# Turning the second half's rows by transposing DMA and a ScalarE weave instead of by TensorE

## The chip, the cores and the metric

The kernel runs on one core of a Trainium2 chip. The metric is the device time of one execution in microseconds (us), taken as the median of several runs: 1520.02 us before the change, over three runs from 1519.76 to 1521.08. One further execution was profiled; every trace number below is from that one.

Engines are named as in the profile: PE is TensorE (matmul; PEld its weight loads), DVE is VectorE, ACT is ScalarE, POOL is GpSimd, and SP is SyncE, which here issues most of the transfers. SPq and ACTq are the instruction queues of SP and ACT, where transfers are issued.

## The reference, cut to what matters

One layer of a hybrid decoder trunk on 1024 tokens of 1024 float32 channels. The first step normalises each token's row and multiplies it by w_in, whose output is cut into eight projections; all of them read the normalised row:

```python
def rms_norm(x, gain):
    y = xf * lax.rsqrt(jnp.mean(xf * xf, axis=-1, keepdims=True) + NORM_EPS)
    return (y * gain.astype(jnp.float32)).astype(x.dtype)

def hybrid_mixer(h, ...):                      # h = rms_norm(x, norm_mix)
    proj = h @ w_in
    xa, ga, q, f, v, g, m_a, m_b = jnp.split(proj, SPLIT_POINTS, axis=-1)
    xa = causal_depthwise_conv(xa, conv_w, conv_b)
    y_a = rg_lru(xa, w_r, b_r, w_i, b_i, lam) * jax.nn.gelu(ga)
    ...                                        # q, f, v: HGRN2 in chunks of 32 tokens, 8 heads of 128
    y = jax.nn.sigmoid(m_a) * y_a + jax.nn.sigmoid(m_b) * y_b
    return y @ w_out
```

Then come a residual sum, a second normalisation, a squared-ReLU MLP of width 4096, another residual and a final normalisation. The change touches only how the normalised rows h of tokens 512 to 1023 get into the layout that the projections read.

## The kernel before

**Layout.** A matmul contracts over the 128 partitions. Rows of x come from memory with tokens on the partitions, so the normalised rows must be turned, channels onto the partitions, before they are multiplied by w_in. The turned rows are held as `hT[c]` for the two token halves c = 0, 1 of 512 tokens each. In float32 each operand is split in two fp32r parts, a high part (an ACT cast, line 97) and a low part (a DVE subtraction, line 101), and a product is three matmuls (`mm3`, line 160). So hT[1] is four tiles: hT10H, hT10L for channels 0 to 511 and hT11H, hT11L for channels 512 to 1023.

**Stages.** The mixers' work is done in eight stages, i = 4c + p for half c and pair p of blocks of 256 channels. Stage i computes v of the pair before (`v_of`), then the projections xa, q and f, and the RG-LRU gates of its own pair, while the HGRN2 chunk work of the pair before is interleaved step by step. The scores of that pair are the short matmuls `sc<-qb,kc` and `sc<-qf,kk` (lines 834 and 845), fed by ACT and DVE. Stage 4 is the first to read hT[1]: its xa projection needs hT10H and hT10L from its first matmuls. All of it sits between about 60 and 500 us of the span; stage 1's xa ends near 75 us, stage 4's begins at 247.7 us.

**Weights.** SP loads each 128x1024 block of weights into one of four `raw` buffers, ACT casts the high part wH, DVE subtracts the low part wL. In the first half wL is also stored to memory (`rest<-wL`), and in the second half reloaded (`wL<-rest`).

**Order.** A scheduler orders the instructions of each engine, guided by the order in which the code calls the pieces, by priorities (`tc.high_priority`) and by added order edges (`held`, line 90, and the like). After that the order on an engine is fixed; an instruction that has to wait holds up all behind it on its engine, and on SP a transfer that has to wait to be issued holds up the transfers behind it.

**The rows of the second half.** Each of the four token tiles of half 1 is loaded and normalised by `next_rows` (line 476): load x (SP), square with sum (ACT, line 185), epsilon (DVE), power (POOL), scale (DVE). Then `transposed` (line 200) turns it: eight PE transposes 128x128 into two banks of PSUM, and `split` writes the high and low parts of both channel halves. Tile 0 is turned after stage 1's xa, tile 1 in stage 2's xa (`hooks` in `stage`), tiles 2 and 3 in stage 3's xa.

## Time and profile before

| what | before |
|---|---|
| median of three runs | 1520.02 us (1519.76 to 1521.08) |
| the profiled execution's own time | 1520.71 us |
| span in the trace | 1518.9 us |
| PE busy | 1508.5 us, 99%, 9035 matmul instructions |
| DVE busy | 1146.9 us, 76% |
| ACT busy | 814.8 us, 54% |
| POOL busy | 155.4 us, 10% |
| PE transposes of `transposed` (line 204) | 32, mean 272 ns each, from 75.6 to 195.9 us |

Busy time is an average over the span. A PE that is busy for nearly all of it says that the other engines' work is hidden behind PE as a whole; where in a stage they are early or late is seen only in the timeline, by comparing when an input is ready with when PE reads it. In a timeline row the columns are start (us), length (us), engine, line, operation, output <- inputs, shape and count; the last bracket, if there is one, is the time that the engine idled before it and what ended that idle time.

### The profile page before, as it was taken

How to read it: one execution, taken by the hardware profiler on the slowest of the kernel's cores; microseconds unless marked ns; L12 is line 12 of the kernel's file. 1: busy time of each engine (PE TensorE's matmuls, PEld its weight loads, DVE VectorE, ACT ScalarE, POOL GpSimd, SP SyncE). 2: the span in 40 equal slices, each digit the busy share in tenths (PEclk: the TensorE clock that was granted, in tenths of full speed). 3: DMA queues.
4: the chain of work that ended last, by engine and by line, in shares of the span. 5: the costliest groups of instructions: out<-in, count | busy, mean ns of one | idle time of the engine just before them, and what ended most of it. 6: DMA issues, size and time to landing. Idle time of an engine off the chain costs nothing.

```text
span 1518.9 us, 23175 instructions
## 1 busy us (share of the span) xinstructions
PE 1508.5 (99%) x9035; PEld 1264.9 (83%) x9035; DVE 1146.9 (76%) x1661; ACT 814.8 (54%) x1369; POOL 155.4 (10%) x191
## 2 busy tenths in 40 slices
PE   9999999999999999999999999999999999999998
PEld 7888988888889888888888888888888888888886
DVE  6889686485585739776756579878888998888877
ACT  5566746656667345645443357666666821111115
POOL 1021120242634600000000000000000000000000
PEclk9999999999999999999999999999999999999999
DMA  7546547466674383442339234666666676666642
GB/s 290 200 176 221 163 171 244 151 230 227 207 241 153 137 307 139 125 139 83 134 116 347 95 125 167 263 249 249 249 249 249 249 278 264 247 249 247 249 184 111
DMA packets 98432, 310.50 MB, mean 204 GB/s; under 512 B 23185, under 2 KB 36625, under 8 KB 85906
## 3 DMA queue, kind: packets, MB, share of 16 engines
q1 hardware_dynamic: 94112, 298.91, 54.4%
q10 hardware_dynamic: 4210, 10.10, 1.8%
q8 instruction: 71, 1.16, 0.3%
q14 instruction: 39, 0.32, 0.1%
HBM read 201.50 MB, written 103.81 MB: 201 GB/s over the span
## 4 chain that ended last, share of the span: by engine, by line
PE 99%; DMA 0%; DVE 0%; ACT 0%; issue 0%; POOL 0%; SPq 0%; POOLq 0%
PE uX L160 11%; PE dX L160 11%; PE gX L160 10%; PE pj_q L160 6%; PE pj_xa L160 6%; PE pj_f L160 6%; PE po L160 6%; PE dY L160 6%; PE uY L160 6%; PE pv L160 5%; PE gY L160 5%; PE uZ L160 3%; PE dZ L160 3%; PE gZ L160 3%; PE g L160 1%; PE mb L160 1%
## 5 line engine op out<-in xcount | busy, mean ns | idle before, releaser
L1916 DVE TENSOR_TENSOR acc<-acc,dX 128x512 f32<-128x512 f32 x128 | 85.1, 684 | 26.7 <-PE dX L160 26.0
L97 ACT CAST wA<-q 128x512 fp32r<-128x512 f32 x46 | 28.6, 622 | 115.9 <-PE dX L160 94.7
L160 PE MATMUL po<-wH,y 128*128 128x512 f32 x256 | 80.6, 391 | 0.0
L101 DVE TENSOR_TENSOR wL<-raw,wH 128x1024 fp32r<-128x1024 f32 x46 | 56.3, 1227 | 31.7 <-ACT wH L97 31.6
L97 ACT CAST wH<-raw 128x1024 fp32r<-128x1024 f32 x46 | 48.1, 1047 | 32.7 <-DMA raw<-wts_in 16.2
L1816 POOL TENSOR_TENSOR gx<-acc,gain 128x256 f32<-128x256 f32 x1 | 0.7, 742 | 604.5 <-DVE acc L1916 604.5
L160 PEld LDWEIGHTS po<-wH,y 128*128 128x128 f32 x256 | 48.1, 188 | 9.8
L1916 DVE TENSOR_TENSOR acc<-acc,dY 128x512 f32<-128x512 f32 x64 | 43.6, 687 | 14.2 <-PE dY L160 13.8
L160 PE MATMUL po<-wL,y 128*128 128x512 f32 x128 | 49.8, 389 | 0.0
L1664 ACT ACTIVATE b<-b 128x512 f32<-128x512 f32 x48 | 30.0, 625 | 29.7 <-DVE b L1663 27.9
L195 POOL TENSOR_TENSOR rstd_h<-rstd_h,mhalf 128x1 f32<-128x1 f32 x8 | 4.3, 545 | 370.2 <-DVE rstd_h L190 370.2
L160 PE MATMUL uX<-h2B11H,wA 128*128 128x512 f32 x128 | 42.1, 390 | 0.0
L101 DVE TENSOR_TENSOR wA<-q,wA 128x512 fp32r<-128x512 f32 x46 | 31.5, 686 | 13.6 <-ACT wA L97 13.6
L606 DVE SCALAR_TENSOR_TENSOR xc<-xp,pvt,xc 128x512 f32<-128x512 f32 x48 | 39.9, 840 | 1.2 <-ACT xc L590 1.1
L123 ACT CAST wH<-raw 128x1024 fp32r<-128x1024 f32 x36 | 37.2, 1044 | 5.6 <-issue 3.1
L160 PE MATMUL gX<-hT00H,wA 128*128 128x512 f32 x112 | 36.8, 390 | 0.0
L1147 DVE TENSOR_TENSOR s<-q,q 128x512 f32<-128x512 f32 x46 | 31.6, 687 | 2.9 <-DMA q<-mlp_in 2.7
L504 POOL TENSOR_TENSOR stt<-r,stt 128x256 fp32r<-128x256 f32 x16 | 21.2, 1348 | 118.8 <-ACT stt L503 107.5
L1155 DVE TENSOR_TENSOR s<-q 128x512 f32<-128x512 f32 x46 | 31.7, 690 | 0.2
L1665 ACT ACTIVATE b<-b 128x512 f32<-128x512 f32 x48 | 30.1, 630 | 1.0
L931 ACT ACTIVATE on<-po 128x128 f32<-128x128 f32 x64 | 16.9, 278 | 24.6 <-PE po L927 24.6
L160 PEld LDWEIGHTS uX<-h2B11H,wA 128*128 128x128 f32 x128 | 24.0, 188 | 5.0
(2328 smaller groups left out, 5285.7 us busy)
## 6 DMA issues: line engine op xcount, KB each, us to landing
q<-mlp_in SPq DMA_DIRECT2D x92, 512.0 KB, 3.6
raw<-wts_in SPq DMA_DIRECT2D x80, 512.0 KB, 4.8
rest<-wL SPq DMA_DIRECT2D x36, 512.0 KB, 3.0
wL<-rest SPq DMA_DIRECT2D x36, 512.0 KB, 4.0
hd<-ri SPq DMA_DIRECT2D x16, 256.0 KB, 3.5
cdT<-stT SPq DMA_DIRECT2D x16, 256.0 KB, 3.1
h<-hd SPq DMA_DIRECT2D x4, 1024.0 KB, 4.7
y<-yd SPq DMA_DIRECT2D x8, 512.0 KB, 9.4
```

The source lines that it names most:

```text
L97: ins = casts[name] = A.copy(h, src)
L101: ins = V.tensor_tensor(out=lo, in0=src, in1=h.bitcast(F32), op=ALU.subtract)
L123: A.copy(h, raw)
L160: ins = PE.matmul(o, a, b, start=begins, stop=ends, **how)
L504: G.tensor_tensor(out=lo, in0=src, in1=h.bitcast(F32), op=ALU.subtract)
L606: ins = V.scalar_tensor_tensor(xc[:, s, :], xp[:, j : j + T], pvt[:, PV_CW + 8 * j + u : PV_CW + 8 * j + u + 1], xc[:, s, :], op0=ALU.mult ...
L931: A.activation(row(s, n), halves_of(po[s][:, n * P : (n + 1) * P]), AF.Square, accum_out=ssq[:, 4 * s + n : 4 * s + n + 1],)
L1147: ins = V.tensor_tensor(out=sa[:, 0, :], in0=a21, in1=a22, op=ALU.add)
L1155: ins = V.tensor_tensor(out=sb[:, 0, :], in0=a21, in1=a11, op=ALU.add)
L1664: A.activation(b[:, at, :], b[:, at, :], AF.Relu, scale=-1.0 if at == 2 else 1.0)
L1665: A.activation(b[:, at, :], b[:, at, :], AF.Square)
L1916: return V.tensor_tensor(out=dst, in0=dst, in1=banks[bk, pr], op=op)
```

## The change

`transposed` is no longer called for these tiles. `next_rows` becomes a generator of four parts that are called one at a time by `row_on(n)`:

1. load x, normalise, and transpose the normalised rows as 2-byte elements by a DMA issued on SP, into a tile `xT`. Each float32 becomes two rows of halves: the low 16 bits and the high 16 bits of one channel stand on separate partitions.
2. store `xT` to memory (`xd`) in two transfers.
3. load it again into `xp` ("parts") in two transfers of 64 partitions, so that both halves of a channel stand on that channel's partition.
4. two ACT copies of 2-byte elements weave the halves back into float32 numbers (`xw`), and `split` writes the high and low parts, now from SBUF.

`xT`, `xw` and the tile that receives x share one buffer (`tile_x`, line 228, tag "xt" with one buffer), so the next tile's x can be loaded only when DVE has read the woven rows of the tile before. `xn` and `xp` share two buffers. The weave is the same operation that the kernel already uses for another tensor at line 1331.

The parts are called at these places: tile 0 at the end of stage 0 (1), in stage 1's xa (2), and in stage 1's q after two steps (3) and after six (4); tile 1 at the end of stage 1 (1), in stage 2's v (2 and 3) and xa (4); tile 2 at the end of stage 2 (1), in stage 3's v (2 and 3) and xa (4); tile 3 in stage 3 before the last steps of f (1 and 2), after the gates (3), and in stage 4's v after its first token tile (4).

```diff
--- before.py
+++ after.py
@@ -148,7 +148,7 @@
         used[0] += 1
         return get_w(used[0] - 1)
 
-    pinned = [False]
+    pinned, newest = [False], [None]
 
     def pin(ins):
         if pinned[0]:
@@ -159,6 +159,7 @@
         for a, b, begins, ends in ((ah, bh, first, False), (ah, bl, False, False), (al, bh, False, last)):
             ins = PE.matmul(o, a, b, start=begins, stop=ends, **how)
             pin(ins)
+            newest[0] = ins
             if chain is not None:
                 edge = mybir.DependencyInfo(mybir.DependencyClass.NoSync, mybir.DependencyReason.DATA)
                 if chain:
@@ -478,7 +479,34 @@
         nc.sync.dma_start(xt, x[(4 + tt) * P : (5 + tt) * P, :])
         xn = xt_pool.tile([P, D], F32, tag="xn", name=f"xn1{tt}", bufs=2)
         norm_rows(xt, xn, gain0[0], f"x1{tt}", behind, square_behind)
-        return xn
+        t = tile_x(f"xT{tt}").bitcast(U16).rearrange("p (j x) -> p j x", x=P)
+        nc.sync.dma_start_transpose(t, xn.bitcast(U16))
+        yield
+        for g in range(2):
+            held(nc.sync.dma_start(xd[tt][:, g], t.rearrange("p (k g) x -> p g k x", g=2)[:, g]), newest[0])
+        yield
+        parts = xt_pool.tile([P, D], F32, tag="xn", name=f"xp1{tt}", bufs=2)
+        parts = parts.bitcast(U16).rearrange("p (h t) -> p h t", h=2)
+        for g in range(2):
+            part = nc.sync.dma_start(
+                parts[64 * g : 64 * g + 64],
+                xd[tt][:, g].rearrange("(a h) k t -> a h (k t)", h=2),
+            )
+            held(part, newest[0])
+        yield
+        whole = tile_x(f"xw{tt}")
+        pairs = whole.bitcast(U16).rearrange("p (t h) -> p h t", h=2)
+        at = slice(tt * P, (tt + 1) * P)
+        with tc.high_priority(400):
+            for h in range(2):
+                cut = slice(h * T, (h + 1) * T)
+                held(A.copy(pairs[:, :, cut], parts[:, :, cut]), newest[0])
+                split(
+                    whole[:, cut].rearrange("p (k t) -> p k t", k=4),
+                    hT[1][0][h][:, :, at],
+                    hT[1][1][h][:, :, at],
+                )
+        yield
 
     def make_combos(i):
         k, cut = i // 2, slice(256 * (i % 2), 256 * (i % 2) + 256)
@@ -949,7 +977,12 @@
         got["normalised"] = normalised
         got["on"] = on
 
-    xn1 = {}
+    xd = [dram.tile([P, 2, 8, P], U16, tag=f"xd{t}", name=f"xd{t}") for t in range(4)]
+    row_parts = {}
+
+    def row_on(n):
+        next(row_parts[n])
+
     where = lambda i: divmod(i, NPAIR)
 
     def hooked(steps, hooks):
@@ -972,9 +1005,8 @@
                 gots[i - 2]["stored"] = on_T(*where(i - 2), gots[i - 2], nc.sync)
             if tt == 3 and i > 1:
                 gots[i - 2]["stored"](nc.scalar.dma_start)
-            for n in {}.get((i, tt), ()):
-                with tc.high_priority(400):
-                    transposed(xn1[n], hT[1], n, f"x1{n}")
+            for n in {(2, 1): (1,), (2, 3): (1,), (3, 1): (2,), (3, 3): (2,), (4, 0): (3,)}.get((i, tt), ()):
+                row_on(n)
 
         yield from v_steps(*where(i - 1), gots[i - 1], between)
 
@@ -984,11 +1016,7 @@
         if i > 1:
             yield from v_of(i)
 
-        def more(n):
-            with tc.high_priority(400):
-                transposed(xn1[n], hT[1], n, f"x1{n}")
-
-        hooks = {at: lambda n=n: more(n) for at, n in {2: ((4, 1),), 3: ((2, 2), (6, 3))}.get(i, ())}
+        hooks = {at: lambda n=n: row_on(n) for at, n in {1: ((6, 0),), 2: ((6, 1),), 3: ((4, 2),)}.get(i, ())}
         px = yield from hooked(project_steps(c, f"xa{c}{p}"), hooks)
         xc, xps = conv_in(c, p, px)
         if i == 0:
@@ -998,20 +1026,24 @@
         yield
         if i == 1:
             gots[0]["tail"]()
-            transposed(xn1[0], hT[1], 0, "x10")
         if i > 4:
             combos_on(2)
 
         def convolve():
             got["xc"] = conv(c, p, xc, xps, None)
 
-        pq = yield from hooked(project_steps(c, f"q{c}{p}"), {} if i == 1 else {6: convolve})
+        hooks = {2: lambda: row_on(0), 6: lambda: row_on(0)} if i == 1 else {6: convolve}
+        pq = yield from hooked(project_steps(c, f"q{c}{p}"), hooks)
         got["q1"] = q_of(c, p, pq)
         yield
         fs = hooked(project_steps(c, f"f{c}{p}"), {6: convolve} if i == 1 else {})
         for _ in range(5 if i > 1 else 7):
             next(fs)
             yield
+        if i == 3:
+            row_parts[3] = next_rows(3, gots[2]["states"])
+            row_on(3)
+            row_on(3)
         if i > 3:
             combos_on(1 if i == 4 else 2)
         if i == 0:
@@ -1023,11 +1055,13 @@
         yield from rg_lru(c, p, got, *got["xc"])
         if i > 0:
             gots[i - 1]["normalised"]()
-        for n in ((0,), (1,), (2, 3))[i] if i < 3 else ():
-            if i == 0:
-                xn1[n] = next_rows(n, behind_first[1], behind_first[0])
-            else:
-                xn1[n] = next_rows(n, gots[0]["states"] if i == 1 else None)
+        if i < 3:
+            row_parts[i] = next_rows(
+                i, behind_first[1] if i == 0 else gots[0]["states"] if i == 1 else None, behind_first[0] if i == 0 else None
+            )
+            row_on(i)
+        if i == 3:
+            row_on(3)
         if i > 1:
             pf = yield from fs
             got["f"], got["kk"] = f_of(c, p, pf)
```

On PE the eight rows `L204 MATMUL xT_x…` are gone and the order is otherwise the same. Three places on the other queues follow. In the names, `wH`, `raw` and `rest` are weight parts as above, `x` is the loaded tile, `xn` the normalised rows, `sq` belongs to the q projection of the stage, `kk`, `kc`, `qb`, `qf` feed the scores of the pair before; line numbers are those of the kernel that the row is from, and differ by about 28 between the two.

ACT in stage 1, before:

```order
L97 CAST hT10H<-xT_x_0_828 128x4x128
L97 CAST hT11H<-xT_x_1_835 128x4x128
L762 COPY seg_721<-seg_721 128x32
L97 CAST wH_911<-raw_909 128x1024
L681 ACT_TABLE_LOAD
L681 ACTIVATE sq_975<-pj_q_0_842 128x512
L97 CAST wH_1043<-raw_1041 128x1024
L681 ACTIVATE sq_975<-pj_q_1_843 128x512
L812 COPY kk_654<-kc_736 128x16x32
L97 CAST xcH_1139<-xc_812 128x1024
L813 COPY qf_1024<-qb_728 128x16x32
L97 CAST wH_1075<-raw_1073 128x1024
```

ACT in stage 1, with the change:

```order
L503 COPY xw_926<-xp_858 128x2x512 x2
L97 CAST hT10H<-xw_926 128x4x128
L97 CAST hT11H<-xw_926 128x4x128
L97 CAST wH_1047<-raw_1045 128x1024
L709 ACT_TABLE_LOAD
L709 ACTIVATE sq_979<-pj_q_0_836 128x512
L709 ACTIVATE sq_979<-pj_q_1_837 128x512
L840 COPY kk_658<-kc_742 128x16x32
L97 CAST xcH_1143<-xc_820 128x1024
L186 ACTIVATE xn_1293,rstd_x_1294<-x_1291 128x1024
L97 CAST wH_1079<-raw_1077 128x1024
L841 COPY qf_1028<-qb_734 128x16x32
```

Ahead of `qf` there are now two weave copies and the square of tile 1's rows (`xn<-x`); the casts of hT follow the weave, and the weight cast `wH_1047`, the table load and both `sq` stand behind them.

SP in stage 1, before (`hd` stores the RG-LRU state rows of a pair):

```order
L129 DMA rest_754<-wL_751 128x1024
L112 DMA raw_1041<-wts_in 128x1024
L129 DMA rest_786<-wL_783 128x1024
L112 DMA raw_1073<-wts_in 128x1024
L129 DMA rest_850<-wL_847 128x1024
L112 DMA raw_1198<-wts_in 128x1024
L670 DMA hd_93<-ri_645 128x512 x2
L129 DMA rest_915<-wL_912 128x1024
L112 DMA raw_1323<-wts_in 128x1024
```

SP in stage 1, with the change:

```order
L486 DMA xd_132<-xT_723 128x8x128
L129 DMA rest_792<-wL_789 128x1024
L486 DMA xd_132<-xT_723 128x8x128
L112 DMA raw_1077<-wts_in 128x1024
L491 DMA xp_858<-xd_132 64x2x1024
L129 DMA rest_844<-wL_841 128x1024
L698 DMA hd_93<-ri_649 128x512 x2
L491 DMA xp_858<-xd_132 64x2x1024
L129 DMA rest_912<-wL_909 128x1024
L112 DMA raw_1202<-wts_in 128x1024
L112 DMA raw_1329<-wts_in 128x1024
L479 DMA x_1291<-x_in 128x1024
```

The two stores to `xd` and the two loads of `xp` are put between the weight transfers, the second load behind both `hd` stores; the load of tile 1's x comes after it.

ACT at the end of stage 3's work and the start of stage 4, before:

```order
L745 COPY kb_2714<-kk_2701 128x512
L662 ACT_TABLE_LOAD
L662 ACTIVATE rw_2630<-rw_2630 128x1024
L123 CAST wH_2745<-raw_2743 128x1024
L123 CAST wH_2869<-raw_2867 128x1024
L762 COPY seg_2711<-seg_2711 128x128
L778 COPY kc_2726<-kb_2714 128x128x2
L782 COPY qb_2718<-qa_2712 128x32x4x2
```

ACT there with the change:

```order
L773 COPY kb_2711<-kk_2698 128x512
L690 ACT_TABLE_LOAD
L690 ACTIVATE rw_2624<-rw_2624 128x1024
L123 CAST wH_2742<-raw_2740 128x1024
L503 COPY xw_2781<-xp_2676 128x2x512 x2
L97 CAST hT10H<-xw_2781 128x4x128
L97 CAST hT11H<-xw_2781 128x4x128
L123 CAST wH_2873<-raw_2871 128x1024
L790 COPY seg_2708<-seg_2708 128x128
L806 COPY kc_2723<-kb_2711 128x128x2
L810 COPY qb_2715<-qa_2709 128x32x4x2
```

Two weave copies and the two casts of hT now stand between the first two casts of reloaded weights, ahead of `seg`, `kc` and `qb`.

## The prediction

> **What bounds the kernel now.** I read the page first: busy share by engine, granted clock, and the chain of work that ended last.
>
> ```profile
> span 1518.9 us, 23175 instructions
> ...
> PE 1508.5 (99%) x9035; PEld 1264.9 (83%) x9035; DVE 1146.9 (76%) x1661; ACT 814.8 (54%) x1369; POOL 155.4 (10%) x191
> ...
> PEclk9999999999999999999999999999999999999999
> ...
> PE 99%; DMA 0%; DVE 0%; ACT 0%; issue 0%; POOL 0%; SPq 0%; POOLq 0%
> ```
>
> The profiled run took 1520.71 us, 1.81 more than its span. TensorE (PE) is busy for 1508.5 us, its granted clock is in the top tenth in every slice, and the chain is PE alone. The next view lists what PE waited for (total, times, longest):
>
> ```profile
> PE gain L336 <- POOL gain_row L326: 2.5, 1, 2.5
> PE xT_x L369 <- DVE xn L360: 0.9, 1, 0.9
> ```
>
> Both waits belong to the kernel's first lines, before the stages. In the stages PE never waits, so only two things move the end: work taken off PE, and a wait that is new for PE. Another engine's work costs something only where its slack before a PE instruction is used up. The change acts in stages 0 to 4, up to about 260 us. One stretch of these, by windows (length, then busy time of PE, PEld, DVE, ACT, POOL, granted clock, DMA share, GB/s):
>
> ```profile
> 60.00:130.00 70.00, 70.00 (x607) 60.14 (x606) 65.40 (x118) 51.20 (x100) 10.10 (x12) 1.00 0.51 174
> ```
>
> DVE is busy for 65 of 70 us and ACT for 51. There is room on average, but both work in order, so what counts is the slack at the places where PE meets them.
>
> **What is removed.** The transposes as a group, then PE's timeline around the first of their four groups:
>
> ```profile
> L204 PE MATMUL xT_x<-ident,xn x32: 270/272/273, 75.6 to 195.9; 128*128 128x128 f32 x32
> ```
>
> ```profile
> 75.10 0.39 PE L160 MATMUL pj_xa<-hT01L,wH 128*128 128x512 f32 x1
> 75.33 0.39 PE L160 MATMUL pj_xa<-hT01H,wL 128*128 128x512 f32 x1
> 75.56 1.03 PE L204 MATMUL xT_x<-ident,xn 128*128 128x128 f32 x8
> 76.35 0.48 PE L160 MATMUL pj_q<-hT00H,wH 128*128 128x512 f32 x1
> 76.67 0.39 PE L160 MATMUL pj_q<-hT00L,wH 128*128 128x512 f32 x1
> ```
>
> A 128x512 matmul normally starts 0.23 us after the one before (75.10, 75.33, 75.56). From 75.33 to 76.67 it is 1.34 us, which holds two normal steps (0.46) and the group: 0.88 us. So 32 transposes in four groups are worth 4 × 0.88 = **−3.5 us**, all of it on the chain. The casts and subtractions that follow a transposition stay; they now read SBUF.
>
> **What is added.** Per token tile a transposing transfer, two stores and two loads on SP's queue, and two ACT copies of 1024 two-byte elements. The nearest rows: the kernel's own weave of another tensor (line 1331, the same operation and shape), then transfers with KB each and median us to landing:
>
> ```profile
> L1331 ACT COPY o<-op x14: 1342/1356/1370, 566.0 to 775.5; 128x1024 uint16<-128x1024 uint16 x14
> ```
>
> ```profile
> wL<-rest SPq DMA_DIRECT2D x36, 512.0 KB, 4.0
> hd<-ri SPq DMA_DIRECT2D x16, 256.0 KB, 3.5
> ```
>
> ```profile
> op<-od SPq DMA_DIRECT2D x6, 512.0 KB, 7.4
> ```
>
> A copy is 1.356 us; two with some overlap at the joint, 2.62. (The Trainium skill, page "ScalarE: Activation LUTs", section "What ACT_TABLE_LOAD costs", gives an ACTIVATE with immediate operands 186 ns + 0.833 ns per element, fp32 and bf16 alike: an estimate of 1.04 us here. The row of line 1331 disagrees by 0.3 us a copy and decides; by the page each stall below would be 0.6 us shorter.) Each of the two loads of woven parts carries 256 KB. The trace has none of them; the nearest are hd at 3.5 us (same size, other direction) and op<-od at 7.4 (same halves on 64 partitions, but 512 KB). I take 3.5 for its size and keep 2.9 to 7.4 for the range, the lower end being 0.6 under hd's median.
>
> The four weaves add 10.5 us to ACT over 190 us. Most of it lands in idle time; it costs where a PE instruction stands behind it.
>
> **Stall A, stage 1 (tile 0).** The second load of the parts stands on SP behind both hd stores, and the weave stands on ACT ahead of everything that the pair before needs for its scores. Before, SP, ACT, DVE and PE at this place:
>
> ```profile
> 83.11 1.51 SPq L670 DMA_DIRECT2D hd<-ri  x2
> ```
>
> ```profile
> 81.88 1.05 ACT L97 CAST wH<-raw 128x1024 fp32r<-128x1024 f32 x1 [0.28 <-PE pj_q L160]
> 82.94 1.28 ACT L681 ACT_TABLE_LOAD   x1
> 88.94 0.60 ACT L681 ACTIVATE sq<-pj_q 128x512 f32<-128x512 f32 x1 [4.72 <-PE pj_q L160]
> ...
> 95.74 0.62 ACT L813 COPY qf<-qb 128x512 f32<-128x512 f32 x1 [1.88 <-DVE qb L704]
> 96.27 1.05 ACT L97 CAST wH<-raw 128x1024 fp32r<-128x1024 f32 x1
> ```
>
> ```profile
> 96.17 0.68 DVE L704 TENSOR_TENSOR qf<-qb,seg 128x512 f32<-128x512 f32 x1
> ```
>
> ```profile
> 97.74 0.69 PE L845 MATMUL sc<-qf,kk 128*64 128x64 f32 x16
> ```
>
> PE's sc<-qf,kk at 97.74 reads ACT's qf (done at 96.36, slack 1.4) and DVE's (96.85, slack 0.9). Without the first group of transposes PE comes at 96.86. Now the chain with the change. The hd issues end at 84.62 (83.11 + 1.51; they wait for DVE's scan, which doesn't move), the load follows and lands at about 88.2. In the meantime ACT has nothing else to do, for the next row in its queue is the weave. From the landing ACT needs, in order, two weaves (2.62), two casts for hT (to 3.6), a weight cast (0.95, to 4.5), the table load (1.28, to 5.8), two sq (to 6.8), kk (to 7.3), xcH (to 8.3), the square of tile 1's rows, the weight cast and qf. Before, the first five of these were over by 84.22 or waited for PE; ACT idled 4.72 us ahead of 88.94, and that cover is now spent on waiting for the load.
>
> The square waits for tile 1's x, and x's buffer is also that of the woven rows: its load starts after DVE's last subtraction, at about 4.5 on the same count. Such a load before, on SP, and its use:
>
> ```profile
> 137.91 0.42 SPq L478 DMA_DIRECT2D x<-x_in  x1
> ```
>
> ```profile
> 143.21 1.06 ACT L185 ACTIVATE xn<-x 128x1024 f32<-128x1024 f32 x1 [2.11 <-DMA x<-x_in]
> ```
>
> From issue to use 5.3 us, with ACT waiting: x would be there at 9.8, 1.5 after ACT. With 4.0, what wL<-rest of the same size takes, ACT hardly waits. The square with its accumulator read takes 1.1, the weight cast 0.95, qf 0.62. So qf is done 11.0 (no wait) to 12.5 us after the landing, at 99.2 to 100.7, and PE waits 2.3 to 3.9 us. I take the middle, **+3.1**. With the parts after 2.9 us and no wait for x it is 1.7; with 7.4 and a wait, 7.8. DVE's own chain (subtractions, kc, a weight, both q behind the late sq, qb, kk, qf) takes 10 us from the landing, so DVE alone would still give 1.3.
>
> **Stages 2 and 3 (tiles 1 and 2).** Here the weave comes early, beside v, and what the change leaves later is a square (tile 3's in stage 3). ACT ahead of stage 3's scores, and PE there:
>
> ```profile
> 208.24 0.62 ACT L812 COPY kk<-kc 128x512 f32<-128x512 f32 x1 [5.52 <-DVE kc L704]
> 209.19 0.62 ACT L813 COPY qf<-qb 128x512 f32<-128x512 f32 x1 [0.34 <-DVE qb L704]
> ```
>
> ```profile
> 211.90 0.69 PE L845 MATMUL sc<-qf,kk 128*64 128x64 f32 x16
> ```
>
> ACT idled 5.52 us before kk, and its qf was done 2.1 us before PE's use. The square (1.06) goes into that idle time. I take 0; with that cover gone it would be up to 1 us.
>
> **Stall B, stage 4 (tile 3).** The weave is queued on ACT behind the first cast of a reloaded weight, and stage 4's first projection reads its result at once. Before, on SP, ACT, DVE and PE:
>
> ```profile
> 236.37 0.33 SPq L124 DMA_DIRECT2D wL<-rest  x1
> ```
>
> ```profile
> 247.12 1.99 ACT L123 CAST wH<-raw 128x1024 fp32r<-128x1024 f32 x2
> ```
>
> ```profile
> 251.26 0.42 DVE L704 TENSOR_TENSOR qb<-qa,seg 128x256 f32<-128x256 f32 x1
> ```
>
> ```profile
> 247.69 0.40 PE L160 MATMUL pj_xa<-hT10H,wH 128*128 128x512 f32 x1
> 247.92 0.40 PE L160 MATMUL pj_xa<-hT10L,wH 128*128 128x512 f32 x1
> ```
>
> Tile 3's parts are loaded behind SP's reload at 236.37, so they are there by 245 even at 7.4 us: no transfer is late here. ACT's first cast ends near 248.1 (247.12 and half of 1.99); ACT has no gap in front of it, since all of its work there follows from PE's gates. Two weaves: 250.7. Cast of hT10H: 251.25. DVE is free at 251.3, its qb now standing behind the subtraction (0.68 for 128x512, as qf above): hT10L is ready at 252.0. PE gets the high part at 251.25 instead of 247.69, does one matmul, and then needs the low part, which it used at 247.92: **+4.1 us**. That all three engines run earlier or later by the terms above changes nothing in the difference. Bounds: 3.5, if a copy were as fast as the weight cast (1.0 in 247.12's row, both f32), and 4.6, if the hand-over between engines costs 0.5 more.
>
> **Sum.** −3.5 + 3.1 + 0 + 4.1 = +3.7 on 1520.71, so 1524.4 for a run like the profiled one. The median of the runs, 1520.02, lies 0.69 below that run; against it I predict **1523.7 us**.
>
> **Rivals.**
> 1. Only stall B. A rests on a load that was never measured and on a slack of about 1 us; should SP pass the parts earlier, or ACT overlap more than I count, A shrinks to 0 to 1.5. Against it: the load is behind the hd stores whatever its speed. +0.6 to +2.1: 1520.6 to 1522.1.
> 2. The transposes' time comes back whole and both stalls are hidden: −3.5, 1516.5. For it: ACT is busy only 51 of 70 us. Against it: B needs nothing to be late, just 2.6 us of copies on an engine without a gap.
> 3. The part loads take 7.4 us, as op<-od does: A is 7.8, so 1528.4. For it: they are issued among weight transfers. Against it: half the size.
> 4. PE's clock falls. B leaves PE idle for 3.5 us in one piece, longer than any wait listed above (2.5). If the matmuls after it ran at half speed for 3.4 us, 1.7 us are lost: 1525.4. No row shows a granted clock below the top tenth, so nothing in the trace speaks for it. (The Trainium skill, page "TensorE: Matmul & The Clock Gate", section "What's actually happening", says that the clock halves after an idle window of about 3.4 us, of a free-running counter, and returns after as long a busy one. B's gap is at the edge of it; no run here shows a gap so long.)
>
> **Chances.** Forecast 0.56, rival 1 0.24, rival 2 0.09, rivals 3 and 4 together 0.11. A measurement of this kernel tells about 0.2% (3.0 us) from no change: faster is below 1517.0, slower above 1523.1. The forecast's own range is 1522.1 (A 1.7, B 3.9) to 1526.1 (A 5.0, B 4.6); a quarter of it, 0.14, lies under 1523.1. So slower is 0.42 + 0.11 = 0.53, same 0.24 + 0.14 = 0.38, faster 0.09. To hold the time 8 times in 10 the range takes in the greater part of rival 1 and the near part of rival 3: 1519.8 to 1527.5.
>
> **What would show it.** PE has 32 instructions fewer and two new waits: sc on ACT's qf, ending near 100 us, of about 3 us, and pj_xa on hT10H and hT10L, ending near 252, of about 4 in two pieces. The copies into the woven rows read 1.36 us, and the idle time before the first is ended by the load of parts. I am wrong if the first wait is missing or is DVE's, if PE waits at a stage between, if the granted clock dips after 252, or if time goes where nothing was moved, past 260 us.

## The result, and the profile after

The changed kernel takes 1528.04 us (median of four runs, 1527.55 to 1529.57) against 1519.89 (1519.73 to 1521.08) for the kernel before on the same chip: a ratio of 1.0054, with a 95% interval of 1.0036 to 1.0071. It is slower by 8.15 us. The prediction was 1523.7 us, so slower by 3.7, and the range ended at 1527.5. The direction was right, the size was not. Two executions with a granted clock far below 1 from end to end, one of sq3_h below (2155.5 us, 0.655) and one of the kernel before (1882.41 us, 0.753), are not in the ratios.

The page of the profiled run (1527.55 us) shows where to begin:

```profile
span 1525.8 us, 23149 instructions
...
PE 1509.0 (99%) x9003; PEld 1263.2 (83%) x9003; DVE 1148.6 (75%) x1661; ACT 824.1 (54%) x1377; POOL 160.3 (11%) x191
...
PEclk9999999999999999999999999999999999999999
...
PE 94%; DVE 2%; ACT 2%; DMA 1%; issue 0%; POOL 0%; SPq 0%; DVEq 0%; ACTq 0%; POOLq 0%
```

PE has 32 instructions fewer and should be busy for 3.5 us less, yet its busy time rose by 0.5 us. The chain of work that ended last, PE alone before, now runs through other engines for 6% of the span. The clock row shows nothing: each of its 40 slices is 38 us long. What PE waited for (total, times, longest):

```profile
PE pj_xa L160 <- ACT hT10H L97: 3.3, 1, 3.3
...
PE sc L873 <- ACT qf L841: 1.7, 1, 1.7
PE sc L862 <- DVE qb L732: 0.9, 1, 0.9
...
PE pkv L924 <- ACT kT L917: 0.4, 1, 0.4
PE pj_xa L160 <- DVE hT10L L101: 0.4, 1, 0.4
PE pk L911 <- ACT scT L884: 0.2, 1, 0.2
```

Both forecast waits are there, sc on qf and pj_xa on hT10H and hT10L. Three others are new: sc on DVE's qb just ahead of the first, and two in stage 3, pkv and pk. Together they are 6.9 us; less 3.5 that makes 3.4, not 8. The rest is seen in windows cut at the edges where the clock changes (length, then busy time of PE, PEld, DVE, ACT, POOL, granted clock, DMA share, GB/s):

```profile
96.58:99.99 3.41, 1.73 (x51) 1.46 (x52) 3.41 (x5) 2.94 (x8) 0.00 (x0) 1.00 0.49 165
99.99:103.40 3.41, 3.41 (x10) 2.62 (x9) 1.66 (x5) 0.00 (x0) 1.96 (x4) 0.50 0.71 256
103.40:106.81 3.41, 3.41 (x24) 3.02 (x24) 0.07 (x1) 2.40 (x6) 0.00 (x0) 1.00 0.13 52
...
250.18:253.59 3.41, 0.87 (x3) 0.51 (x4) 3.41 (x9) 3.41 (x5) 0.00 (x0) 1.00 1.02 390
253.59:257.00 3.41, 3.41 (x10) 2.63 (x9) 3.41 (x8) 2.23 (x8) 3.15 (x1) 0.50 1.04 405
257.00:260.41 3.41, 3.41 (x16) 2.80 (x15) 3.41 (x5) 0.24 (x1) 3.41 (x3) 1.00 0.49 195
```

After each of the two stalls TensorE's granted clock is 0.50 for 3.41 us. PE counts as busy there, which is most of why its busy time did not fall. PE's timeline has both stalls and the pace after them:

```profile
96.53 0.46 PE L862 MATMUL sc<-qb,kc 128*32 128x32 f32 x32 [0.86 <-DVE qb L732]
98.66 0.69 PE L873 MATMUL sc<-qf,kk 128*64 128x64 f32 x16 [1.68 <-ACT qf L841]
...
100.57 0.63 PE L160 MATMUL pj_f<-hT01L,wH 128*128 128x512 f32 x1
100.99 0.63 PE L160 MATMUL pj_f<-hT01H,wL 128*128 128x512 f32 x1
...
252.36 0.50 PE L160 MATMUL pj_xa<-hT10H,wH 128*128 128x512 f32 x1 [3.25 <-ACT hT10H L97]
253.22 0.50 PE L160 MATMUL pj_xa<-hT10L,wH 128*128 128x512 f32 x1 [0.36 <-DVE hT10L L101]
```

After the first stall steps are 0.42 us apart (100.57 to 100.99) where 0.23 is normal: about half speed.

**The account by stages.** Take each stage from the start of its xa projection to the start of the next one's. A stage with no transposes and no wait is 59.82 us long (stage 2 with the change, stage 4 before). The table gives what each of stages 1 to 4 took beyond that, in us, in the profiled executions; the later stages of these two kernels agree.

| kernel | stage 1 | stage 2 | stage 3 | stage 4 | sum |
|---|---|---|---|---|---|
| before | 0.88 | 0.89 | 1.78 | 0.00 | 3.55 |
| the change | 4.28 | 0.00 | 4.80 | 2.37 | 11.45 |

Before, the excess is the four groups of transposes and nothing else. With the change it is: stage 1, waits of 2.68 and 1.6 lost at half speed; stage 3, 1.39 lost at pk and pkv, and 3.41 waiting for hT10H; stage 4, 0.64 waiting for hT10L and 1.7 lost at half speed. The difference is +7.9 us. (The spans differ by 6.9 only because the profiled execution before reached stage 1's xa 0.86 us later; the medians differ by 8.15.)

ACT's timeline shows the three places that cause it:

```profile
87.72 2.59 ACT L503 COPY xw<-xp 128x1024 uint16<-128x1024 uint16 x2 [6.56 <-DMA xp<-xd]
...
208.94 1.06 ACT L186 ACTIVATE xn<-x 128x1024 f32<-128x1024 f32 x1 [6.36 <-DMA x<-x_in]
...
248.36 1.03 ACT L123 CAST wH<-raw 128x1024 fp32r<-128x1024 f32 x1
249.30 2.53 ACT L503 COPY xw<-xp 128x1024 uint16<-128x1024 uint16 x2
```

In stage 1 ACT stands 6.56 us for the woven parts, and qf is late. In stage 4 the weave follows the weight cast without a gap, and hT10H is late. In stage 3 ACT stands 6.36 us for tile 3's x, with kk and qf behind it: this was not forecast.

### The profile page after: what moved, and what is told of

Same layout as the page of the kernel before. It is cut to its first block, busy times and chain, and to the rows that moved or that the text cites. A ratio compares the mean times of both kernels' runs of the same rounds, so it can differ in the third digit from the quotient of the medians.

```text
span 1525.8 us, 23149 instructions
## 1 busy us (share of the span) xinstructions
PE 1509.0 (99%) x9003; PEld 1263.2 (83%) x9003; DVE 1148.6 (75%) x1661; ACT 824.1 (54%) x1377; POOL 160.3 (11%) x191
## 4 chain that ended last, share of the span: by engine, by line
PE 94%; DVE 2%; ACT 2%; DMA 1%; issue 0%; POOL 0%; SPq 0%; DVEq 0%; ACTq 0%; POOLq 0%
PE uX L160 11%; PE dX L160 11%; PE gX L160 10%; PE po L160 6%; PE dY L160 6%; PE uY L160 6%; PE pj_xa L160 5%; PE gY L160 5%; PE pj_f L160 5%; PE pv L160 5%; PE pj_q L160 4%; PE uZ L160 3%; PE dZ L160 3%; PE gZ L160 2%; PE g L160 1%; PE mb L160 1%
```

## The experiments

Ratios are against the kernel before, run on the same chip beside them (medians 1520.11, 1520.06 and 1520.28 in the three groups). Diffs are against the changed kernel. The excess over 59.82 us by stage is the key to all of them. Each row is one profiled execution, and that can lie anywhere among the runs of its kernel: early's is one of the shortest of ten, sq3_s's the longest of eight.

| kernel | stage 1 | stage 2 | stage 3 | stage 4 | sum |
|---|---|---|---|---|---|
| fill (with its spare matmuls) | 2.72 | 0.00 | 0.49 | 4.24 | 7.45 |
| t0_pe | 0.88 | 0.00 | 4.89 | 3.11 | 8.88 |
| early3 | 4.10 | 2.44 | 0.68 | 0.00 | 7.22 |
| early | 1.03 | 1.83 | 0.68 | 0.00 | 3.54 |
| t12 | 0.88 | 4.16 | 1.95 | 0.00 | 6.99 |
| early_b | 0.24 | 0.49 | 0.00 | 0.00 | 0.73 |
| t3_pe2 | 4.09 | 5.40 | 1.93 | 0.00 | 11.42 |
| fill_b8 (with its spare matmuls) | 5.50 | 0.00 | 1.69 | 5.80 | 12.99 |
| sq3_s | 4.22 | 0.00 | 0.11 | 4.87 | 9.20 |
| early_b5 | 0.28 | 0.00 | 0.00 | 0.00 | 0.28 |

The theory after the result: the two stalls cost what was forecast, stage 3 has a third, and each of the two large stalls makes the clock fall. The first rival: the slow stretches have another cause (transfers, or the load on all engines), so they would stay if PE were kept busy. The second: the time lies in the order of ACT's copies alone, and a better order returns it.

### Spare matmuls in both stalls

Eleven spare matmuls at the scores in stage 1 (`spare`: four ahead of sc<-qb,kc and seven ahead of sc<-qf,kk), fourteen before stage 4's xa. Their results are overwritten.

```diff
+                if name == "xa10" and half == 0 and k == 0:
+                    for _ in range(14):
+                        pin(PE.matmul(pp[0], wh[:, 0:P], hT[0][0][0][:, 0, :], start=True, stop=True))
...
+        spare(4)
...
+        spare(7)
```

> The change with spare matmuls on TensorE where it would wait (11 in stage 1, 14 at the start of stage 4, 128x512 each, their result overwritten); nothing else moves. Theory: the two stalls also let the granted clock fall to half for some 3.4 us each, which costs 1.6 and 1.7 us in the trace of the change; with TensorE kept busy the clock stays and the waits remain: 3.3 us less than 1528.0, about 1524.7, granted clock 1.00 in both stretches. Rival, the slow stretches have another cause (the transfers or the new copies): 1528.0 and the clock falls as before.

Measured: 1524.46 us (1523.21 to 1529.82), ratio 1.0026 (1.0013 to 1.0039). Its windows:

```profile
60.00:130.00 70.00, 70.00 (x602) 59.77 (x601) 64.56 (x117) 52.31 (x100) 11.52 (x12) 1.00 0.65 198
...
190.00:260.00 70.00, 69.31 (x655) 58.45 (x654) 56.94 (x105) 47.06 (x88) 17.48 (x17) 1.00 0.79 240
```

The clock is 1.00 over the stretches that hold both stalls, although ACT, DVE and the transfers do much as they did: the weave is still late at both places, and only the wait is filled with work. So the slow stretches come from PE standing idle, and by the medians filling PE is worth 3.6 us of the 8 (1528.04 less 1524.46); the traces put 1.6 and 1.7 on the two slow stretches. The first rival falls.

### Tile 0 back on TensorE

The transposition is called after stage 1's xa, as before the change.

```diff
+        if tt in (0,):
+            yield
+            with tc.high_priority(400):
+                transposed(xn, hT[1], tt, f"x1{tt}")
+            yield
+            return
...
-        hooks = {at: lambda n=n: row_on(n) for at, n in {1: ((6, 0),), 2: ((6, 1),), 3: ((4, 2),)}.get(i, ())}
+        hooks = {at: lambda n=n: row_on(n) for at, n in {2: ((6, 1),), 3: ((4, 2),)}.get(i, ())}
...
+            row_on(0)
...
-        hooks = {2: lambda: row_on(0), 6: lambda: row_on(0)} if i == 1 else {6: convolve}
+        hooks = {} if i == 1 else {6: convolve}
```

> Tile 0 turned by TensorE again (stage 1 as before the change), tiles 1 to 3 by transfers. Theory: stage 1's waits (2.7 us) and the slow stretch after them (1.6) go, one group of transposes (0.88) comes back: 3.4 us less than 1528.0, about 1524.6, and no clock below 1.00 near 100 us. Rival, the slow stretch is not tied to the wait: 1526.2. Stall and slow stretch at stage 4 stay as they are by both.

Measured: 1526.18 us (1523.69 to 1526.77), ratio 1.003 (1.002 to 1.004). Stage 1 is what it was before the change (excess 0.88, the group of transposes), with no wait and a clock of 1.00. So stall A, its wait and its slow stretch, comes from tile 0's way alone. The time came out 1.6 above the theory's number and at the rival's, but not for the rival's reason. Windows of t0_pe around stage 4's start:

```profile
244.00:247.41 3.41, 1.10 (x10) 0.90 (x8) 3.41 (x6) 3.41 (x4) 0.00 (x0) 1.00 1.06 305
247.41:250.82 3.41, 2.40 (x5) 1.60 (x6) 3.41 (x9) 3.41 (x8) 0.97 (x1) 0.50 1.02 388
250.82:254.24 3.42, 3.42 (x10) 2.65 (x9) 3.42 (x6) 0.98 (x4) 3.42 (x2) 0.50 1.01 397
```

The clock fell while PE was still waiting, and stayed low for 6.83 us, twice as long as in the change. A fall there cost 2.9 us in place of 1.7. The same wait has two prices, and the section on the hardware says why. That is 1.2 of the 1.6; this execution was also 1.8 us longer behind stage 4 than the change's, with two waits there that the change does not have (dX for a load of u4n, 0.7, and uX, 0.4).

### Tile 3 and tile 2 earlier

Tile 3's steps are called earlier, so that its weave is done long before stage 4 (its copies ran at 226.4 and 229.1 us, stage 4's xa began at 250.5); tile 2 moves up with it.

```diff
-            for n in {(2, 1): (1,), (2, 3): (1,), (3, 1): (2,), (3, 3): (2,), (4, 0): (3,)}.get((i, tt), ()):
+            for n in {(2, 1): (1,), (2, 3): (1,), (3, 0): (2,), (3, 2): (3,)}.get((i, tt), ()):
...
-        hooks = {at: lambda n=n: row_on(n) for at, n in {1: ((6, 0),), 2: ((6, 1),), 3: ((4, 2),)}.get(i, ())}
+        hooks = {at: lambda n=n: row_on(n) for at, n in {1: ((6, 0),), 2: ((6, 1),), 3: ((6, 3),)}.get(i, ())}
...
+        if i == 3:
+            hooks = {4: lambda: row_on(3), 6: convolve}
+        if i == 2:
+            row_parts[2] = next_rows(2, None)
+            row_on(2)
```

> Tile 3's chain starts earlier (tile 2's steps are called in stage 2, tile 3's from the v of stage 3 on), so that its weave is done on ScalarE before stage 4; tile 0 as in the change. Theory: the wait at stage 4 (4.0 us) and its slow stretch (1.7) go: 1522.3. Rival, the slow stretch is not tied to it: 1524.0. If ScalarE's new place for tiles 2 and 3 makes TensorE wait in stage 3, more than that, with a wait there on kk or qf.

Measured: 1525.15 us (1523.41 to 1530.6), ratio 1.0027 (1.0012 to 1.0042), 2.9 us above the theory's number, which had allowed for new waits in stage 3. Stall B and its slow stretch are gone whole: stage 4's excess is 0.00, and 3.41 less waits in stage 3. What is late next, by the list of waits: pv, the projection v, on ACT's kk, 1.6, since tile 2's weave now stands on ACT ahead of f and kk; sc on DVE's qf in stage 2, 0.5; pk in stage 3, 0.5. The gain of 5.8 us at stage 4 (4.05 and 1.7) was partly given back at places that had been free.

### Tile 0 earlier too

As early3, with tile 0's stores and loads four steps earlier in stage 1 and its weave three, so that the second load no longer stands behind the hd stores:

```diff
-        hooks = {at: lambda n=n: row_on(n) for at, n in {1: ((6, 0),), 2: ((6, 1),), 3: ((4, 2),)}.get(i, ())}
+        hooks = {at: lambda n=n: row_on(n) for at, n in {1: ((2, 0), (6, 0)), 2: ((6, 1),), 3: ((6, 3),)}.get(i, ())}
...
-        hooks = {2: lambda: row_on(0), 6: lambda: row_on(0)} if i == 1 else {6: convolve}
+        hooks = {3: lambda: row_on(0)} if i == 1 else {6: convolve}
```

> As early3, and tile 0's stores and loads are called earlier too, so that its weave does not wait behind the hd stores. Theory: both stalls and both slow stretches go, the 3.5 us of transposes come back whole: 1516.4, faster than before by 0.2%. Rival, stalls gone but slow stretches not tied to them: 1519.7. If tile 1's square (it waits for x) holds ScalarE too long in stage 1, a rest of up to 1 us there: 1517.4.

Measured: 1521.85 us (1519.68 to 1526.15), ratio 1.0008 (0.9995 to 1.0021): not to be told from the kernel before, and 4 to 5 us above what was expected. What its PE waited for in the stages (total, times, longest):

```profile
PE pv L160 <- ACT kk L723: 1.6, 1, 1.6
PE sc L873 <- DVE qf L732: 0.7, 1, 0.7
PE pk L911 <- DVE kk L732: 0.5, 1, 0.5
```

ACT's timeline of the same kernel in stage 1:

```profile
88.88 1.06 ACT L186 ACTIVATE xn<-x 128x1024 f32<-128x1024 f32 x1 [4.60 <-DMA x<-x_in]
```

Stall A's 2.68 has shrunk to 0.7, and in the profiled execution (1519.73 us) there is no slow stretch in any of the four stages. What is left in stage 1 is not the weave but the square of tile 1's rows, which held ACT for 4.60 us until x had come: the same fault as in stage 3 of the change. The wait of 1.6 for kk is the weave of tile 2 again. Both are orders on ACT that the next version mends.

### Only tiles 1 and 2 by DMA

Tiles 0 and 3 on TensorE, 1 and 2 as in the change, to price the middle alone.

```diff
+        if tt in (0, 3):
+            yield
+            with tc.high_priority(400):
+                transposed(xn, hT[1], tt, f"x1{tt}")
+            yield
+            return
...
-        if i == 3:
+        if i == 2:
+            row_parts[3] = next_rows(3, None)
             row_on(3)
+            row_on(2)
```

> Only tiles 1 and 2 by transfers and weave; tiles 0 and 3 turned by TensorE in stages 1 and 3. Theory: the loss comes from the two places where a weave stands in front of what TensorE needs next, so with these two gone only the two removed groups are left, -1.8 us against the kernel before: 1518.2, no wait of TensorE over 0.3 us in stages 1 to 4 and the clock at 1.00 throughout. Rival, transfers and weaves cost something wherever they stand: 1520 or more.

Measured: 1523.65 us (1521.44 to 1524.51), ratio 1.0021 (1.0012 to 1.0031), 5 us above the expectation. This was a miss of the experiment, not of the theory: the edit put the normalisation of tile 3 into stage 2 before the last of the scans' products. DVE's timeline there:

```profile
158.24 0.15 DVE L191 TENSOR_SCALAR rstd_x<-rstd_x 128x1 f32<-128x1 f32 x1 [1.27 <-ACT xn L186]
...
159.06 1.28 DVE L197 SCALAR_TENSOR_TENSOR xn<-x,rstd_x,gain 128x1024 f32<-128x1024 f32 x1 [0.41 <-POOL rstd_x L196]
```

And PE's:

```profile
161.21 0.68 PE L960 MATMUL po<-v,scT 128*128 128x128 f32 x4 [2.29 <-DVE sn L944]
```

DVE stood 1.27 us for ACT's square and 0.41 for POOL's power, the scale then took 1.28, and sn, which PE's po needs, stood behind. PE lost 2.45 us there, and the clock fell after it for 3.42 us (161.86 to 165.27, 0.50), another 1.7. With tiles 1 and 2 alone the first and fourth stages are as before the change, which was to be seen; the price of the middle was not measured cleanly.

### Both moves, and two orders on ACT mended

As early, with tile 1's square behind the pair's scores and tile 2's weave behind f and kk:

```diff
-            for n in {(2, 1): (1,), (2, 3): (1,), (3, 1): (2,), (3, 3): (2,), (4, 0): (3,)}.get((i, tt), ()):
+            for n in {(2, 1): (1,), (2, 3): (1,), (3, 2): (2,), (3, 3): (3,)}.get((i, tt), ()):
...
-                i, behind_first[1] if i == 0 else gots[0]["states"] if i == 1 else None, behind_first[0] if i == 0 else None
+                i, behind_first[1] if i == 0 else gots[0]["states"] if i == 1 else None, behind_first[0] if i == 0 else gots[0]["halved"]
```

> All four tiles by transfers, begun early as in the kernel early, but tile 1's square stands behind the scores of stage 1 (it held ScalarE until x had landed, and TensorE's sc waited 1.0 us), and tile 2's weave stands behind the f and kk of its stage (TensorE's v waited 1.7 us for them). Theory: what is left is a wait of 0.6 us in stage 3 (pk on DVE's kk): -3.5 + 0.6 against the kernel before, 1517.0. Rival, the woven copies are now in front of seg, kc and qb, and TensorE waits for these at sc in stage 3 instead: 1518 to 1519.

Measured: 1517.33 us (1516.52 to 1517.71), ratio 0.9981 (0.9972 to 0.999). Expected was 1517.0. All the waits are gone but two of 0.2 and 0.4 us, as the sum of 0.73 in the table says. The same transfers, copies and bytes per tile that cost 8 us in the change cost almost nothing here: only their places differ. So the second rival is true as far as it goes: a better order returns the time, and with the waits the slow stretches go too.

### Tile 3 on TensorE, tiles 0 to 2 by DMA

The edit is t12's, with `tt in (3,)`, and stage 1 left as in the change.

> Tile 3 alone turned by TensorE again (in stage 3, its x loaded in stage 2), tiles 0 to 2 by transfers as in the change. Theory: the wait at stage 4 (4.0), its slow stretch (1.7) and the waits of pk and pkv in stage 3 (1.3, ScalarE held by tile 3's x there) go, 0.9 of transposes comes back: 1528.0 - 6.1 = 1521.9, stage 1 as in the change. Rival, the waits in stage 3 are the weave's doing: 1523.2.

Measured: 1527.17 us (1525.07 to 1528.48), ratio 1.0045 (1.003 to 1.006), 5 us above the expectation. It repeats t12's fault, since it has the same edit in stage 2: po waited 3.5 us for sn, and the clock fell after it for 3.42 us. What it does show is the other end: with tile 3 off the DMA way, stage 4's excess is 0.00, no wait and no slow stretch, while stage 1 has its 4.09 as in the change. So stall B, its wait and its slow stretch, comes from tile 3, as stall A does from tile 0.

### Eight spare matmuls at stage 4 only

The first part of fill's edit with `range(8)`, one execution: how much of the wait has to be filled.

> The change with 8 spare matmuls (1.8 us) at the start of stage 4, nothing in stage 1: the wait for hT10H and hT10L stays 4.0 us, but TensorE is idle for only some 2.2 of them. Theory, the clock falls by how long TensorE is idle within about 3.4 us: early was idle for 1.7 at one place without a fall, the change in stage 1 for 2.7 with one, so 2.2 lies between; a fall shows as matmuls of 0.43 us after the wait and 1.7 us more. Rival, it falls wherever a wait of 4 us ended, however busy TensorE was in it: a fall as in the change.

Measured: 1529.95 us in one run. PE idles 1.5 and 0.3 us in place of 3.3 and 0.4, and the clock falls all the same. Windows of fill_b8 at stage 1 and at stage 4:

```profile
94.57:97.98 3.41, 1.50 (x37) 0.92 (x35) 3.41 (x7) 3.41 (x6) 0.00 (x0) 1.00 0.94 298
97.98:101.39 3.41, 2.73 (x20) 2.33 (x21) 3.41 (x6) 1.54 (x6) 0.26 (x1) 0.50 0.26 105
101.39:104.81 3.42, 3.42 (x9) 2.64 (x9) 0.25 (x1) 0.00 (x0) 1.70 (x4) 0.50 0.72 252
...
251.58:254.99 3.41, 1.62 (x6) 0.84 (x5) 3.41 (x9) 3.41 (x5) 0.00 (x0) 1.00 1.01 394
```

In the 3.41 us before the fall at 254.99 PE was busy for 1.62, idle for 1.79. Stage 1, untouched by this edit, has the change's two waits (0.9 and 1.7), but here the slow stretch took 6.83 us, and stage 1 was 1.2 us longer than in the change. So the size of the slow stretch differs from execution to execution with the same waits. A fall at stage 4 is also what the rival of the expectation said, a fall after any wait of 4 us however busy PE was; fill speaks against that rival, for there PE was kept busy through such a wait and the clock stayed.

### Tile 3's square at two other places

In stage 3 of the change the square of tile 3's rows stands ahead of kk and waits for x. One more argument puts it later, behind the pair's scores (sq3_h, the diff) or, with `gots[2]["states"]` in its place, behind the pair's states (sq3_s):

```diff
-            row_parts[3] = next_rows(3, gots[2]["states"])
+            row_parts[3] = next_rows(3, gots[2]["states"], gots[2]["halved"])
```

> The change with one row moved on ScalarE: the square of tile 3's rows stands behind the second sq of stage 3, ahead of kT, not ahead of kk and qf. Theory: the 1.3 us that TensorE waits at pk and pkv in stage 3 come from ScalarE being held until tile 3's x lands; with the square behind kk and qf the waits at pk go, and since the square (1.1 us) now stands ahead of kT, whose slack was 0.5, pkv waits some 0.6: 1528.0 - 0.7 = 1527.3, the stalls of stages 1 and 4 and their slow stretches as in the change. Rival, the waits come from the woven copies at the start of stage 3: no change, 1528.0.

> The same with the square behind kT and scT; the scheduler then also puts tile 3's weave ahead of the weight cast, of rw and of kb at the end of stage 3. Theory: the waits of pk and pkv in stage 3 go (1.3), and the wait at stage 4 is set by the landing of the parts instead of by ScalarE's queue: landing near 246, 3.7 us of weave, cast and subtraction, so a wait of 1.5 to 2.5 in place of 4.0, too short to bring the clock down if 2.1 us of idle time is about what it takes: 1528.0 - 1.3 - 2.0 - 1.7 = 1523. With a fall of the clock 1524.7. Rival, what was ahead of the weave (rw, the v copy) is now late for TensorE in stage 4 and gives the time back: 1526 or more.

Measured for the first: 1526.68 us (three runs, 1525.52 to 1527.4), ratio 1.0042 (1.0027 to 1.0058), where 1527.3 was expected and the change has 1528.04. Runs of one kernel lie further apart than that in other groups, and no trace of this kernel can be set beside the others, so whether stage 3's waits went is not known. It decides nothing.

For the second: 1525.3 us (1523.06 to 1527.27), ratio 1.0032 (1.0022 to 1.0042), where the theory's numbers were 1523 and 1524.7. Stage 3's excess is 0.11, where the change has 1.39 beside the wait for hT10H: the waits at pk and pkv went with the square that held ACT for x. The rest of the expectation was off, since the scheduler moved more than the square, and what its rival named, a late copy of v, is what the trace shows. The largest wait of sq3_s:

```profile
PE pj_xa L160 <- ACT v L581: 2.7, 1, 2.7
```

ACT's timeline of sq3_s ahead of it:

```profile
244.88 2.64 ACT L503 COPY xw<-xp 128x1024 uint16<-128x1024 uint16 x2 [0.16 <-DMA xp<-xd]
...
251.81 0.37 ACT L581 COPY v<-pv 128x256 f32<-128x256 f32 x1
```

The weave now comes before the weight cast, and it ends 4 us earlier than in the change. But it and its two casts also stand ahead of the copy of v, and PE, a few matmuls into xa, waited 2.7 us for that, after which the clock fell again. A weave of 2.6 us ahead of anything that PE needs soon makes PE wait, whichever copy is the late one.

### The best version, measured longer

The kernel of early_b in five rounds.

> The kernel early_b once more, in five rounds: 1517.3, faster than the kernel before by 0.1 to 0.25%, the clock at 1.00 in stages 1 to 4.

Measured: 1516.9 us (1516.34 to 1518.82, eleven runs) against 1520.28, ratio 0.998 (0.9972 to 0.9989): faster than the kernel before by 0.2%, and than the change by 11 us. All that PE waited for in the whole run:

```profile
PE gain L337 <- POOL gain_row L327: 2.5, 1, 2.5
PE xT_x L370 <- DVE xn L361: 0.2, 1, 0.2
PE sc L873 <- PE sc L862: 0.2, 1, 0.2
```

The weave's copies as a group (ns: shortest, median, longest; first and last start):

```profile
L503 ACT COPY xw<-xp x8: 1352/1360/1392, 79.7 to 221.0; 128x1024 uint16<-128x1024 uint16 x8
```

The first two waits lie ahead of the stages, as before. The copies are as long as in the change (1.36 us), and from 79.7 to 221.0 they lie where PE waits for nothing behind them. The excess is 0.28 us where the kernel before has 3.55: −3.27, nearly all of the transposes' time.

## Why the prediction was right or wrong

**The bound** was incomplete: work taken off PE and new waits of PE moved the end, as it said, but so did a third thing, PE's own speed after a wait. That stood only among the rivals.

**Removed, −3.5: right.** Stage 2 of the change, with its group gone and nothing new, is 59.82 us; before it was 60.71.

**The price of a weave, 1.356 us a copy: right.** The eight copies of the change as a group:

```profile
L503 ACT COPY xw<-xp x8: 1331/1354/1381, 87.7 to 250.5; 128x1024 uint16<-128x1024 uint16 x8
```

Its loads of parts among the transfers (KB each, median us to landing):

```profile
xp<-xd SPq DMA_DIRECT2D x8, 256.0 KB, 4.1
```

The median copy is 1354 ns, so the choice of the kernel's own weave over the estimate of 1.04 us was right. The loads of parts took 4.1 us, where 3.5 was taken; the one that stall A hangs on took 3.84.

**Stall A, +3.1: right in size, 2.68.** The mechanism is as forecast: ACT stood for the parts (6.56 us, ended by xp<-xd) and the chain to qf followed. The doubt over x fell on the short side: x was there when the square's turn came, at 96.00. The wait came in two pieces, not one. DVE's qb was late too, for 0.93 us, as the bound for DVE alone (1.3) suggested; ACT's qf added 1.75.

**Stages 2 and 3, 0: wrong for stage 3.** This step said that the square goes into ACT's idle time of 5.52 us before kk. The idle time was there; the square had nothing to work on. Its chain:

```profile
202.78 0.11 SPq L698
...
202.98 5.93 DMA x<-x_in
...
217.67 0.66 PE pk L911 x4
```

And DVE's timeline behind the square's row, from the same execution:

```profile
212.10 1.23 DVE L101 TENSOR_TENSOR wL<-raw,wH 128x1024 fp32r<-128x1024 f32 x1 [1.20 <-ACT wH L97]
```

The load of x stands on SP behind the hd stores of line 698 and was issued at 202.98; it landed 5.93 us later, and kk, qf and a weight cast followed the square. DVE stood 1.20 us for that cast, and what pk needs came later by it. The cost was 1.39 us. The prediction named the price of a lost cover as up to 1 us, and used for stage 1 the very argument (a load behind hd, an engine that stands for it) that was missing here. Three executions with this same order on ACT show the cause, since the cost goes with the time at which x lets the square begin, counted from stage 3's xa: 20.30 us in fill, where stage 3 lost 0.49; 21.20 in the change, 1.39; 21.46 in fill_b8, 1.69 (in fill and fill_b8 the spare matmuls take the wait for hT10H out of stage 3). In sq3_s, with the square out of the way, it is 0.11.

**Stall B, +4.1: right, 4.05.** 3.41 for the high part and 0.64 for the low, in the forecast's order, with no transfer late. One detail was off at no cost: the second load of the parts was issued at 241.64 and landed 5.4 us later, at 247.0, not by 245; ACT's turn for the weave came only at 249.30. t3_pe2 shows that it is tile 3's.

**The clock: wrong.** This is the step that failed most. The sum had no term for it; the fourth rival gave it to stall B only, at 1.7 us, and shared a chance of 0.11 with the third. It happened at both stalls, 1.6 and 1.7 us, and fill shows that idle time of PE causes it. The prediction gave a fall only to a gap in one piece, longer than any wait that the trace before had (2.5 us); A's longest piece is 1.68 us. The sentence "nothing in the trace speaks for it" took a lack of cases for evidence: before the change PE doesn't wait in the stages at all.

**The sum.** Forecast −3.5 + 3.1 + 0 + 4.1 = +3.7; measured −3.5 + 2.7 + 1.4 + 4.05 + 3.3 = +7.9. Of the 4.2 us missing, 3.3 are the clock and 1.4 stage 3; stall A gave back 0.4. The rivals that had stall A hidden, or both, fell. The second, that the transposes' time comes back whole, is false for the change and true of the mechanism: early_b and early_b5 show it, once each weave stands at a place of ACT where nothing behind it is due.

**What stays open:** the spread of single times. Runs of one kernel lie 3 us apart in t0_pe (1523.69 to 1526.77) and 7 in early3 (1523.41 to 1530.6), and in that same group the kernel before had five of thirty runs between 1522.17 and 1526.21. The mean granted clock, which every run has on record, goes with a part of it: in early3 it is 0.998 in the runs up to 1524.66, 0.997 or less from 1525.64 on and 0.995 in the longest, and one slow stretch of 3.41 us takes off 0.001 (half of 3.41 in some 1520). It doesn't go with all of it: fill has 0.999 at 1523.21 and at 1527.43. What else spreads the times is not known, since only one execution of each kernel has a trace; medians that are 2 or 3 us apart say less here than the accounts by stage.

## What to carry to other kernels

When work moves from a full engine to a half-empty one, price the place and not the average: list what is queued behind the new instruction on its in-order engine, and ask for every instruction that waits for a transfer, the moved ones too, when that transfer can be issued at all. A stall of TensorE has a second price: in these traces, where it stood idle for about half of a window of 3.4 us, the next window ran at half speed, and short waits in one window counted together (1.5 and 0.3 in fill_b8). If the first version loses, look at where the copies stand before giving up the idea: here the same instructions in other places went from 8 us slower to 3.4 faster.

## What the hardware showed that was not expected

**The granted clock is set on a fixed grid, by how busy TensorE was in the window before.** In the traces with a fall every slow stretch is 3.41 to 3.42 us long or twice that (6.83), and two falls in one execution are a whole number of 3.413 us apart: 99.99 and 253.59 in the change (153.60, 45 windows), 98.92 and 167.19 in t3_pe2 (68.27, 20 windows), 97.98 and 254.99 in fill_b8 (157.01, 46 windows), 99.37 and 252.97 in sq3_s (153.60, 45 windows). With the grid laid through a fall and the windows view cut on it, PE's idle time and the clock of the window after were:

| kernel | window from, us | PE idle, us of 3.41 | the next window's clock |
|---|---|---|---|
| the change | 93.16 | 0.85 | 1.00 |
| t3_pe2 | 160.36 | 1.05 | 1.00 |
| the change | 246.76 | 1.06 | 1.00 |
| early3 | 185.24 | 1.58 | 1.00 |
| early | 181.86 | 1.58 | 1.00 |
| the change | 96.58 | 1.68 | 0.50 |
| fill_b8 | 251.58 | 1.79 | 0.50 |
| fill_b8 | 94.57 | 1.91 | 0.50 |
| t12 | 158.45 | 2.29 | 0.50 |
| the change | 250.18 | 2.54 | 0.50 |
| t3_pe2, already slow | 98.92 | 0.43 | 1.00 |
| fill_b8, already slow | 97.98 | 0.68 | 0.50 |
| t0_pe, already slow | 247.41 | 1.01 | 0.50 |

So in these traces the clock falls once about half of a window is idle (between 1.58 and 1.68 us; the ends of matmuls in a trace are modelled, so the bound is no finer), and a slow clock comes back after a window with less idle time than some bound between 0.43 and 0.68. A fall costs half of 3.41 us, 1.7, and about 3 where the next window still holds a piece of the stall (t0_pe 2.9, stage 1 of fill_b8 2.8). Where the grid lies against the program differs between executions, so the same stall costs once (stage 1 of the change) or twice (stage 1 of fill_b8); by the rule it could also lie across an edge and not bring the clock down at all, which no trace here shows. In early's stages nothing fell, but its clock falls at 1513.06, at the end of the program, and 390 windows of 3.413 us before that is an edge at 181.86: its gap of 1.58 us lay whole in one window and brought no fall, as in early3.

The Trainium skill, page "TensorE: Matmul & The Clock Gate", section "What's actually happening", gives a free-running window of 3413 ns; the falls agree to 0.01 us. It also says that the clock is halved after at least one idle window. The traces differ here: a window in which PE was busy for 1.73 of 3.41 us was enough, and that is what the prediction had wrong when it looked for one long gap.
